# A row-wise NaN-ignoring maximum: the last tiles divided anew, and the number-free rows of 358 columns marked behind tile 52 instead of 414 behind tile 60

## The chip, the cores and the metric

The kernel runs on one core of a Trainium2 chip. The metric is the device time of one execution in microseconds (us). The core's engines work side by side and meet only at semaphores: VectorE (DVE in the profile), ScalarE (ACT), GpSimd (POOL) and SyncE (SP), which here only issues DMAs. TensorE has no work.

## The reference

```python
batch, seq, dim = 32, 2048, 2048
x = np.random.randn(batch, seq, dim).astype(np.float32)
mask = np.random.rand(batch, seq, dim) < 0.1
x[mask] = np.nan
...
return np.nanmax(x, axis=axis).astype(np.float32)     # axis = -1
```

A tenth of the 134 million elements is NaN; each of the 65,536 rows of 2048 elements gives the maximum of its numbers, and NaN if it has none. 537 MB are read, 0.26 MB written.

## The kernel before

Every one of the 128 partitions handles 512 rows. A **unit** is a quarter of a row, `Q` = 512 elements of each partition. The table `TILES` lists 74 tiles, one entry `(loads, pieces, reds)` each, all in units: the first tile has 4 units (one row), each other 28 (seven rows). The tiles go in turn through three load buffers `xt` (`BUFS`).

Each tile passes four stages.

- **Load.** SP issues one DMA for each number in `loads`. The first of them waits until the last reduction of the tile three before it has freed the buffer. Each DMA also waits for the landing of the DMA 14 before it (`LANES`).
- **Keys.** For each entry of `pieces`, ACT reads the upper 16 bits of the elements and writes a key of 16 bits into one of three key buffers `kt` (`e_key = act(...)`; the page shows it as "ACTIVATE kt<-xt"). The function has two slopes and sends every NaN to a key that later becomes a very low number.
- **Way back.** The keys are turned into upper halves again and written over the originals in `xt`. A positive number in `pieces` gives this to POOL (`pool(...)`, "TENSOR_SCALAR xt<-kt"), a negative one to ACT (`release()`, "ACTIVATE xt<-kt"). An entry in parentheses is one key step with several ways back. A negative number written as a float (`-2.0`) lets ACT make the next key first.
- **Reduction.** DVE takes the maximum over the row (`tensor_reduce`, "TENSOR_REDUCE acc<-xt") of as many units as the next number of `reds` says, as soon as all their ways back are done. The maxima of a partition stand in `acc`, one column for each row.

So `([28], [6, 10, 12], [16, 12])` is one load of 28 units, three key steps with three ways back on POOL, and reductions of four rows and of three. `([14, 14], [9, -4, 4, 4, 7], [12, 8, 8])` is two loads, and the second way back (4 units) is ACT's.

Every engine works through its instructions in the order in which the Python loop emits them; there is no planner behind it, the table is the plan. `Order` keeps the semaphores: each instruction waits only for what its engine has not yet seen. Where a reduction needs one last way back of POOL and one of ACT, `joints()` finds the two, and both then count on one semaphore of their own (`pair74_5`), so that the reduction waits once. Tiles whose number stands in `APART` are left out of that.

A row without a number ends as a very low constant in `acc` (`NONE`). `find()` marks such rows by two passes over a range of `acc`: a comparison (`none`), then an OR that makes them NaN. The tiles are split into six `GROUPS`, and a group's columns form one block of the output with one store. The marking is done behind the groups in `FLAGGED`, over all columns since the last one; group 4 (`LATE`) is marked by POOL at the very end, the last group, tile 74, by DVE. The stores of groups 0 to 3 are issued after the last load; those of groups 4 and 5 wait for their marking.

Of the kernel before, what the change touches and what calls it, by code (L numbers as in the profile page):

```python
# [15 lines left out]
TILES = (  # L16
    [([4], [4], [4])]
    + [([28], [7, 9, 12], [16, 12])] * 7
    + [([28], [9, 12, -7], [8, 20])]
    + [([28], [7, 9, 12], [16, 12])] * 7  # L20
    + [([28], [9, 12, -7], [8, 20])]
    + [([28], [7, 9, 12], [16, 12])] * 7
    + [([28], [9, 12, -7], [8, 20])]
    + [([28], [7, 9, 12], [16, 12])] * 7
    + [([28], [9, 12, -7], [8, 20])]
    + [([28], [7, 9, 12], [16, 12])] * 7
    + [([28], [9, 12, -7], [8, 20])]
    + [([28], [7, 9, 12], [16, 12])] * 7
    + [([28], [6, 10, 12], [16, 12])] * 3
    + [([28], [7, 9, 12], [16, 12])]  # L30
    + [([28], [6, 10, 12], [16, 12])] * 3
    + [([28], [7, 9, 12], [12, 16])] * 2
    + [([28], [7, 10, 11], [12, 16])]
    + [([28], [6, 10, 12], [16, 12])] * 3
    + [([28], [8, 11, 9], [8, 8, 12])]
    + [([20, 8], [11, -6, 6, 5], [16, 12])]
    + [([20, 8], [12, (-4, 7), 5], [8, 8, 12])]
    + [([17, 11], [12, (-4, 6), 6], [4, 12, 12])]
    + [([16, 12], [11, -5, 5, 7], [16, 12])]
    + [([13, 15], [9, -4, 7, 8], [12, 8, 8])]  # L40
    + [([14, 14], [9, -4, 4, 4, 7], [12, 8, 8])]
    + [([11, 10, 7], [5, 6, (-3, 7), 7], [4, 4, 4, 8, 8])]
    + [([11, 9, 8], [4, 7, (-2, 7), 6, -2], [4, 4, 4, 8, 8])]
    + [([8, 7, 6, 7], [3, 5, 7, (3, -3), 3, 4], [8, 4, 8, 8])]
    + [([6, 5, 6, 5, 6], [5, (5, -1), (-1, 5), 5, 3, 3], [4, 4, 4, 4, 4, 4, 4])]
    + [([5, 6, 5, 4, 4, 3, 1], [(-2, 3), 3, 3, (4, -1), 4, 4, -2.0, 2], [4, 4, 3, 1, 4, 4, 4, 4])]
    + [([4, 4, 3, 2, 4, 2, 3, 3, 3], [2, 2, 4, (-2.0, 1), 2, 3, 3, (-1, 2), (1, -1, 1), 2, -1.0], [4, 4, 4, 4, 4, 4, 4])]
)

GROUPS = [TILES[i : i + 15] for i in range(0, 60, 15)] + [TILES[60:73], TILES[73:]]  # L50


FLAGGED = (3, 5)
LATE = 4

APART = (70, 71, 72, 73)
WIDE = 7
BUFS = 3

# [23 lines left out]
def joints(pieces, reds):  # L83

    flat = []  # L90
    at = 0
    for step, parts in enumerate(pieces):
        for c in parts if isinstance(parts, tuple) else (parts,):

            flat.append((at, at + abs(c), c < 0, step + isinstance(c, float)))
            at += abs(c)
    needs = []
    done = 0
    for n in reds:
        over = [i for i, (a, b, _, _) in enumerate(flat) if a < done + n and b > done]  # L100
        done += n
        pools = [i for i in over if not flat[i][2]]
        backs = [i for i in over if flat[i][2]]
        if pools and backs and flat[pools[-1]][3] > flat[backs[-1]][3]:
            backs = []
        needs.append(pools[-1:] + backs[-1:])
    pairs = {}
    for need in needs:
        if len(need) == 2 and all(sum(i in n for n in needs) == 1 for i in need):
            for i in need:  # L110
                pairs[i] = tuple(need)
    return pairs
# [61 lines left out]
def kernel(  # L174
# [28 lines left out]
    of = out.bitcast(i32).flatten_outer_dims().rearrange("r c -> (r c)")  # L203
    rows = [sum(sum(loads) for loads, _, _ in g) * Q // D for g in GROUPS]
    assert R == P * sum(rows)
# [14 lines left out]
    with tc.tile_critical():  # L220
# [25 lines left out]
        def find(who, engine, deps, acc, none, op):  # L246
            e = order.add(
                who,
                engine,
                lambda: engine.tensor_scalar(  # L250
                    out=none,
                    in0=acc,
                    scalar1=NONE,
                    scalar2=float(0x00800000),
                    op0=ALU.is_equal,
                    op1=ALU.mult,
                ),
                deps,
            )
            bits = acc.bitcast(i32)  # L260
            return order.add(
                who,
                engine,
                lambda: engine.tensor_tensor(  # L264
                    out=bits, in0=bits, in1=none, op=op
                ),
                [e],
            )
# [14 lines left out]
        number = 0  # L283
# [5 lines left out]
        r0 = 0  # L289
        for gi, (s, g) in enumerate(zip(rows, GROUPS)):  # L290
            xg = xr[r0 : r0 + P * s].rearrange("(p s) d -> p (s d)", p=P)
# [5 lines left out]
            for loads, pieces, reds in g:  # L297
# [5 lines left out]
                for c in loads:  # L303
                    c *= Q
                    a, b = at, at + c
# [18 lines left out]
                part = []  # L324
                held = []
                pairs = {}
                if number not in APART:
                    pairs = joints(pieces, [n // Q for n in reds])
                flat = sum((p if isinstance(p, tuple) else (p,) for p in pieces), ())
                half = {}  # L330
# [114 lines left out]
            else:  # L445
# [3 lines left out]
                ready += [e] * (gi + 1 - len(ready))  # L449
            if gi == len(GROUPS) - 1:  # L450
                e = find("pool", nc.gpsimd, late_after, late_acc, late, ALU.add)
# [50 lines left out]
```

## Time and profile before

| | |
|---|---|
| median of 3 runs | 1251.56 us (1251.53 to 1252.36) |
| profiled execution | 1251.85 us, its span 1250.1 us |
| DVE busy | 1110.8 us (89%), 181 instructions |
| ACT busy | 965.5 us (77%), 273 instructions |
| POOL busy | 1168.7 us (93%), 242 instructions |
| read from HBM | 536.87 MB, 430 GB/s over the span |
| load of a 28-unit tile (7168 KB) | 22.6 us from issue to landing, one about every 16.9 us |

The span runs from the first to the last instruction; the execution's time also holds what lies around it, here 1.75 us. Times within a profile are counted from the start of the span. "Idle before, and who ended it" beside an instruction is the time for which its engine stood still just before it.

Three engines and the DMA queue are all close to full, so shares of the whole span say little about the end: they must be read by stretch.

### The profile page before, as it was taken

How to read it: one execution, taken by the hardware profiler on the slowest of the kernel's cores; microseconds unless marked ns; L12 is line 12 of the kernel's file. 1: busy time of each engine (PE TensorE's matmuls, PEld its weight loads, DVE VectorE, ACT ScalarE, POOL GpSimd, SP SyncE). 2: the span in 40 equal slices, each digit the busy share in tenths (PEclk: the TensorE clock that was granted, in tenths of full speed). 3: DMA queues.
4: the chain of work that ended last, by engine and by line, in shares of the span. 5: the costliest groups of instructions: out<-in, count | busy, mean ns of one | idle time of the engine just before them, and what ended most of it. 6: DMA issues, size and time to landing. Idle time of an engine off the chain costs nothing.

```text
span 1250.1 us, 886 instructions
## 1 busy us (share of the span) xinstructions
DVE 1110.8 (89%) x181; ACT 965.5 (77%) x273; POOL 1168.7 (93%) x242
## 2 busy tenths in 40 slices
DVE  0788989888889888898988888988888999999999
ACT  3777887778777877788777877777777778999998
POOL 2999989998999899998999899999999999989998
DMA  9999999999999999999999999999999999999997
GB/s 415 435 417 440 440 440 429 422 441 440 435 420 437 440 437 433 422 440 440 437 429 426 440 440 433 422 437 440 437 433 422 441 437 423 438 431 429 428 428 311
DMA packets 15991, 537.20 MB, mean 430 GB/s; under 512 B 2544, under 2 KB 2544, under 8 KB 3568
## 3 DMA queue, kind: packets, MB, share of 16 engines
q1 hardware_dynamic: 15984, 537.14, 99.4%
q14 instruction: 7, 0.06, 0.0%
HBM read 536.87 MB, written 0.26 MB: 430 GB/s over the span
## 4 chain that ended last, share of the span: by engine, by line
DMA 40%; DVE 29%; POOL 22%; ACT 9%; issue 1%; SPq 0%
DMA xt<-in_x_dram 40%; DVE acc L244 29%; POOL xt L237 22%; ACT kt L227 8%; ACT xt L227 1%; SPq L309 0%; DVE none L250 0%; DVE acc L264 0%; SPq L465 0%; SPq L220 0%
## 5 line engine op out<-in xcount | busy, mean ns | idle before, releaser
L237 POOL TENSOR_SCALAR xt<-kt 128x3584 int16<-128x3584 uint16 (+11 forms) x236 | 1167.6, 4948 | 77.6 <-ACT kt L227 63.5
L244 DVE TENSOR_REDUCE acc<-xt 128x3 f32<-128x6144 f32 (+4 forms) x175 | 1107.5, 6379 | 136.6 <-POOL xt L237 129.2
L227 ACT ACTIVATE kt<-xt 128x3584 uint16<-128x3584 int16 (+9 forms) x247 | 913.4, 3734 | 278.3 <-DMA xt<-in_x_dram 258.1
L227 ACT ACTIVATE xt<-kt 128x512 int16<-128x512 uint16 (+6 forms) x24 | 52.9, 2203 | 0.7
L227 ACT ACT_TABLE_LOAD x1 | 1.3, 1283 | 0.9 <-SPq L220 0.9
L244 DVE TENSOR_REDUCE xt<-xt 128x1 f32<-128x1536 f32 x1 | 1.7, 1742 | 0.0
L270 DVE MEMSET scalars<- 128x1 f32 x1 | 0.1, 59 | 1.0 <-SPq L220 1.0
L250 DVE TENSOR_SCALAR none<-acc 128x414 int32<-128x414 f32 (+1 forms) x2 | 0.8, 380 | 0.1
L264 DVE TENSOR_TENSOR acc<-acc,none 128x414 int32<-128x414 int32 (+1 forms) x2 | 0.7, 374 | 0.1
L250 POOL TENSOR_SCALAR late<-acc 128x91 int32<-128x91 f32 x1 | 0.5, 547 | 0.1
L264 POOL TENSOR_TENSOR acc<-acc,late 128x91 int32<-128x91 int32 x1 | 0.3, 341 | 0.1
L483 POOL MEMSET const-float32-0.0<- 128x1 f32 x1 | 0.1, 99 | 0.2 <-issue 0.2
L227 ACT ACTIVATE scalars<-scalars 128x1 f32<-128x1 f32 x1 | 0.2, 203 | 0.0
L483 POOL MEMSET const-bfloat16-1.0<- 128x1 bf16 x1 | 0.1, 102 | 0.0
L483 POOL MEMSET const-uint8-127<- 128x1 uint8 x1 | 0.1, 102 | 0.0
L483 POOL MEMSET const-float32-1.0<- 128x1 f32 x1 | 0.1, 99 | 0.0
## 6 DMA issues: line engine op xcount, KB each, us to landing
xt<-in_x_dram SPq DMA_DIRECT2D x61, 7168.0 KB, 22.6
xt<-in_x_dram SPq DMA_DIRECT2D x2, 5120.0 KB, 17.5
xt<-in_x_dram SPq DMA_DIRECT2D x3, 2816.0 KB, 22.7
xt<-in_x_dram SPq DMA_DIRECT2D x4, 2048.0 KB, 22.3
xt<-in_x_dram SPq DMA_DIRECT2D x5, 1536.0 KB, 29.1
xt<-in_x_dram SPq DMA_DIRECT2D x2, 3584.0 KB, 24.7
xt<-in_x_dram SPq DMA_DIRECT2D x6, 1024.0 KB, 26.8
xt<-in_x_dram SPq DMA_DIRECT2D x3, 1792.0 KB, 30.0
```

The lines of the kernel that those rows point to most:

```text
L227: lambda: nc.scalar.activation(**kw),
L237: lambda: nc.gpsimd.tensor_scalar(**kw),
L244: return order.add("dve", nc.vector, lambda: do(**kw), deps)
L250: lambda: engine.tensor_scalar(out=none, in0=acc, scalar1=NONE, scalar2=float(0x00800000), op0=ALU.is_equal, op1=ALU.mult,),
L264: lambda: engine.tensor_tensor(out=bits, in0=bits, in1=none, op=op),
L270: e_top = order.add("dve", nc.vector, lambda: nc.vector.memset(top, EDGE), [])
L483: nc = _bacc.Bacc("TRN2", target_bir_lowering=False, num_devices=1)
```

## The change

The rows of the table from tile 49 on are replaced. The loads of 28 units stay whole up to tile 63 (before, up to tile 62); the last tile has 12 loads instead of 9, all in all there are 107 loads instead of 105. More tiles carry ways back on ACT, among them tile 52 and tiles 57 to 66. The groups are cut at tiles 13, 26, 39, 52 and 73 instead of 15, 30, 45, 60 and 73: their columns are 85, 91, 91, 91, 147 and 7 instead of 99, 105, 105, 105, 91 and 7. So DVE marks the first 358 columns behind tile 52, where it marked 414 behind tile 60, and POOL marks 147 columns at the end instead of 91. `APART` is replaced by `PAIRED`, a list of the tiles that do use the common semaphore.

```diff
-    + [([28], [7, 9, 12], [16, 12])] * 7
-    + [([28], [6, 10, 12], [16, 12])] * 3
-    + [([28], [7, 9, 12], [16, 12])]
-    + [([28], [6, 10, 12], [16, 12])] * 3
-    + [([28], [7, 9, 12], [12, 16])] * 2
-    + [([28], [7, 10, 11], [12, 16])]
-    + [([28], [6, 10, 12], [16, 12])] * 3
-    + [([28], [8, 11, 9], [8, 8, 12])]
-    + [([20, 8], [11, -6, 6, 5], [16, 12])]
-    + [([20, 8], [12, (-4, 7), 5], [8, 8, 12])]
-    + [([17, 11], [12, (-4, 6), 6], [4, 12, 12])]
-    + [([16, 12], [11, -5, 5, 7], [16, 12])]
-    + [([13, 15], [9, -4, 7, 8], [12, 8, 8])]
-    + [([14, 14], [9, -4, 4, 4, 7], [12, 8, 8])]
-    + [([11, 10, 7], [5, 6, (-3, 7), 7], [4, 4, 4, 8, 8])]
-    + [([11, 9, 8], [4, 7, (-2, 7), 6, -2], [4, 4, 4, 8, 8])]
-    + [([8, 7, 6, 7], [3, 5, 7, (3, -3), 3, 4], [8, 4, 8, 8])]
-    + [([6, 5, 6, 5, 6], [5, (5, -1), (-1, 5), 5, 3, 3], [4, 4, 4, 4, 4, 4, 4])]
-    + [([5, 6, 5, 4, 4, 3, 1], [(-2, 3), 3, 3, (4, -1), 4, 4, -2.0, 2], [4, 4, 3, 1, 4, 4, 4, 4])]
-    + [([4, 4, 3, 2, 4, 2, 3, 3, 3], [2, 2, 4, (-2.0, 1), 2, 3, 3, (-1, 2), (1, -1, 1), 2, -1.0], [4, 4, 4, 4, 4, 4, 4])]
+    + [([28], [7, 9, 12], [16, 12])] * 10
+    + [([28], [9, 7, -1, 11], [16, 8, 4])]
+    + [([28], [7, 10, (2, 9)], [16, 12])] * 2
+    + [([28], [7, 10, (9, 2)], [16, 12])]
+    + [([28], [9, 8, (2, 9)], [16, 12])]
+    + [([28], [10, (-2, 5), 11], [8, 8, 12])]
+    + [([28], [7, (-5, 7), 9], [16, 12])]
+    + [([28], [7, (-3, 9), 9], [16, 12])]
+    + [([28], [7, (-5, 7), 9], [16, 8, 4])]
+    + [([28], [(6, 6), (5, -6), 5], [12, 16])]
+    + [([28], [9, 10, -4.0, 2, 3], [8, 8, 12])]
+    + [([28], [5, 5, 8, 6, (3, -1.0)], [4, 4, 4, 4, 8, 4])]
+    + [([17, 11], [8, (-3, 9), 8], [8, 12, 8])]
+    + [([17, 11], [8, 8, 7, -5], [4, 4, 8, 12])]
+    + [([17, 11], [8, 8, 9, -3], [8, 8, 12])]
+    + [([12, 16], [(8, -2.0), 2, 8, 8], [8, 4, 8, 8])]
+    + [([14, 14], [8, -3.0, 3, 6, 8], [8, 4, 8, 8])]
+    + [([11, 9, 8], [8, -2, 5, 5, (7, -1)], [8, 4, 8, 8])]
+    + [([10, 10, 8], [8, (-1, -1), 5, 5, (6, -2)], [8, 4, 8, 8])]
+    + [([9, 7, 4, 8], [4, (-2.0, 3), (3, 2), 2, 4, (3, -1.0), 4], [4, 8, 8, 8])]
+    + [([8, 7, 6, 7], [4, 4, 4, 3, (-2, 4), 3, 4], [4, 4, 4, 4, 4, 4, 4])]
+    + [([5, 3, 5, 3, 4, 3, 2, 3], [3, (-1, 4), 4, 4, 4, 3, -2, 3], [4, 4, 4, 4, 4, 4, 4])]
+    + [([4, 3, 1, 1, 3, 3, 2, 1, 3, 2, 2, 3], [4, 3, (-1, 1), 3, 3, -1.0, 2, 2, 3, (-1, 1), 2, -1.0], [4, 4, 4, 4, 4, 4, 4])]
...
-GROUPS = [TILES[i : i + 15] for i in range(0, 60, 15)] + [TILES[60:73], TILES[73:]]
+BOUNDS = (0, 13, 26, 39, 52, 73, 74)
+GROUPS = [TILES[a:b] for a, b in zip(BOUNDS, BOUNDS[1:])]
...
-APART = (70, 71, 72, 73)
+PAIRED = (33, 41, 57, 58, 59, 60, 64, 65, 66, 67, 68, 73, 74)
...
-                if number not in APART:
+                if number in PAIRED:
                     pairs = joints(pieces, [n // Q for n in reds])
```

## The prediction

> **What bounds the kernel now.** I began with the share of the windows, because the change touches only the stretch from tile 49 on. Columns: window, its length, busy time of VectorE (DVE), ScalarE (ACT) and GpSimd (POOL) with instructions, clock, DMA share, GB/s.
>
> ```profile
> 700.00:1038.00 338.00, 303.18 (x42) 247.84 (x60) 327.87 (x60) 1.00 1.00 434
> 1038.00:1141.00 103.00, 102.51 (x19) 97.81 (x30) 95.39 (x20) 1.00 1.00 433
> 1141.00:1204.00 63.00, 63.00 (x19) 58.37 (x26) 60.27 (x19) 1.00 1.00 429
> 1204.00:1249.00 45.00, 44.43 (x24) 39.04 (x31) 40.54 (x24) 1.00 0.86 357
> ```
>
> Up to 1204 the DMA share is 1.00: the loads set the pace and no schedule of the engines can beat them. The last load lands at 1242.63. What the engines still owe then is the part a new division can move: from there to the end of the span (1250.09) it is 7.46 us. In the last two windows DVE has no idle time either, and POOL little. The timeline tells how little (start, length, engine, operation, count, idle before it and who ended that):
>
> ```profile
> 1058.80 162.77 DVE L244 TENSOR_REDUCE acc<-xt 128x3 f32<-128x6144 f32 x40 [0.42 <-POOL xt L237]
> ...
> 1126.27 9.06 POOL L237 TENSOR_SCALAR xt<-kt 128x3584 int16<-128x3584 uint16 x2 [2.25 <-ACT kt L227]
> ...
> 1135.60 5.33 POOL L237 TENSOR_SCALAR xt<-kt 128x4608 int16<-128x4608 uint16 x1 [0.27 <-ACT kt L227]
> ...
> 1141.93 61.72 POOL L237 TENSOR_SCALAR xt<-kt 128x2048 int16<-128x2048 uint16 x19 [1.01 <-ACT kt L227]
> ...
> 1204.22 32.83 POOL L237 TENSOR_SCALAR xt<-kt 128x2560 int16<-128x2560 uint16 x16 [0.57 <-ACT kt L227]
> ...
> 1237.27 8.41 POOL L237 TENSOR_SCALAR xt<-kt 128x1536 int16<-128x1536 uint16 x6 [0.23 <-ACT kt L227]
> ```
>
> POOL waits for ACT by 0.27, 1.01, 0.57 and 0.23 us after 1126, and 0.12 once more inside the run of 19; otherwise its conversions stand 0.079 us apart. So POOL is two microseconds from being a second bound. Its prices in that stretch (groups by form, mean ns of one):
>
> ```profile
> L237 POOL TENSOR_SCALAR xt<-kt 128x3584 int16<-128x3584 uint16 x7 | 29.4, 4198 | 2.7 <-ACT kt L227 2.2
> L237 POOL TENSOR_SCALAR xt<-kt 128x2048 int16<-128x2048 uint16 x8 | 19.8, 2479 | 1.6 <-ACT kt L227 1.0
> L237 POOL TENSOR_SCALAR xt<-kt 128x1536 int16<-128x1536 uint16 x10 | 19.1, 1906 | 1.0 <-ACT kt L227 0.2
> L237 POOL TENSOR_SCALAR xt<-kt 128x2560 int16<-128x2560 uint16 x6 | 18.3, 3048 | 1.0 <-ACT kt L227 0.6
> ```
>
> The other widths have rows of the same kind: 4.772 us for 8 units (one unit is 512 elements), 3.625 for 6, 1.334 for 2, 0.765 for 1. That is about 0.571 a unit and 0.195 an instruction. Last, the end of the chain of waits: DVE, released by POOL, runs to the end.
>
> ```profile
> 1237.07 5.57 DVE acc L244 x3
> 1243.66 0.67 DVE acc L244
> 1244.33 1.52 issue
> 1245.86 2.29 DVE acc L244
> ```
>
> **The change, part by part.**
>
> *POOL's work, tiles 53 to 66.* Counting units in the table, POOL has 1964 of 2048 before and 1951 after; ACT takes 97 back instead of 84. POOL has 247 conversions instead of 236. Over the whole kernel that is 13 x 0.571 - 11 x (0.195 + 0.079) = 4.4 us less for POOL. But it comes off tiles 53 to 60 (224 units before, 209 after), where the DMA share is 1.00: worth nothing at the end.
>
> *POOL's work, tiles 67 to 74.* Here it goes the other way: tiles 68 to 74 have 170 units in 42 conversions before, 174 in 44 after, that is 4 x 0.571 + 2 x 0.274 = 2.8 us more. To see whether the waits above absorb it, I carried the durations through the new order of each engine. The load that ends tile 67 lands at 1122.98, as before (tile ends stay where they are, and the loads run without a gap). ACT converts 8 units of it in 3.61 (row of 4096), and POOL starts at 1126.70. From there POOL has 46 conversions, 2 of tile 67 and 44 of tiles 68 to 74: 6 of 8 units, 1 of 7, 2 of 6, 4 of 5, 13 of 4, 13 of 3, 5 of 2, 2 of 1. By the rows: 28.63 + 4.20 + 7.25 + 12.20 + 32.20 + 24.78 + 6.67 + 1.53 = 117.46, and 45 gaps of 0.079 make 121.0. In my carried order ACT is always ahead of it (closest at 1147, by 0.05 us; elsewhere by 0.46 us or more), so POOL never waits and ends at 1247.71. Before, it ended at 1245.69: 2.0 us later.
>
> *DVE at the end.* The elements to reduce are the same and so is DVE's total after 1141 (106.9 us, 107.0 before, each reduction less its 0.083 of overlap with the next). It is now DVE that waits, in eight places by 0.10 to 0.35 us; with the overlaps lost there, about 2 us in all. The last wait is for the conversion that completes row 5 of tile 74, four from POOL's last: 1247.71 - 1.91 - 0.77 - 1.33 - 0.24 = 1243.47. Then come three reductions of one row at 2.276 each, two of them overlapping by 0.083: 1243.55 + 6.66 = 1250.21, against 1248.13 before. The pieces for rows 6 and 7 are ready 0.15 to 0.2 us before DVE is.
>
> *Marking of number-free rows.* The two DVE passes move from 1032.86 (414 columns, 0.592 + 0.586) to behind tile 52, near 897.7, with 358 columns: in proportion 0.53 + 0.53. They fit in the wait for POOL that precedes the next tile's first reduction (1.7 us at every tile), so nothing. If that cover were gone, 1.1 us would go to the release of a load buffer, below. While the old pair ran, POOL's conversion of 5120 elements took 5.912 against 5.910 in the mean row: no contention. The Trainium skill, "SBUF — State Buffer", section "SBUF: two separate sides", has VectorE and GpSimd exclude each other over a shared port pair for some VectorE forms. By that rule 1.1 us could be added to POOL near 898; the row says it does not apply to these two passes.
>
> *The late group.* POOL's two passes at the very end have 147 columns, not 91. Rows: 0.547 + 0.341 for 91; between that and 147/91 of it, 0.9 to 1.4. They begin after 1247.7 and are over by 1249.3, their store issued by 1249.7; the last store can only start at 1250.6. Covered by 0.9 us.
>
> *Loads and stores.* Two more loads, 0.43 us of SP issue each, with 10 or more loads queued ahead: nothing. A short load costs little more than its bytes (768 KB landed 1.88 us after the one before; at 434 GB/s it is 1.81), so 0.14 us, and POOL's last conversion has 2.6 us of slack to its load. The pairs of waits (`PAIRED`) change which semaphore a reduction waits for; the nearest row is an extra wait instruction of 0.02 us on DVE, before conversions that end later anyway.
>
> *Sum.* Last reduction ends 1250.21 instead of 1248.13: +2.1 us. What follows (marking of 7 columns, store, end: 1.96) is unchanged. The profiled execution took 1251.85 with a span of 1250.1, so it goes to 1253.9; the median of the runs is 0.3 below that execution, so **1253.6**.
>
> **Rivals.** About 0.2% (2.5 us) is what a measurement of this kernel can tell from no change; the forecast, +2.1, lies within.
>
> *Slower: loads come late after tile 52.* A load starts when the tile three before it is reduced. Today it is issued 5.0 us (982.42 for a landing at 987.42) or more before the load ahead of it lands, and no gap follows. In the new order the issue slips: by my sums to 4.8 at tile 55, then 4.2, 4.1, 4.2 and 4.0, since four conversions of a 28-unit tile (4.20 + 5.91 + 1.33 + 5.34 and four gaps, 17.1 us) are longer than its load (16.9). The very first load took 4.99 from issue to landing, 2.5 of it for its bytes, so about 2.5 should be enough and the margin holds. If the queue needs 5.0, up to 1.0 us of DMA time is lost once, everything behind slides with it, and the time is 1254.6; it passes 2.5 us from a loss of 0.4. A wait of ACT that my sums put 0.05 us away adds to the same side.
>
> *No change: DVE remains the bound.* If POOL's conversions stay ahead of DVE, DVE's 106.9 us give the old end, 1251.6. For it: DVE had no idle time before. Against: POOL's own sum ends 2 us later.
>
> *Faster.* The conversions before tile 68 leave POOL 4.4 us less; were the tail POOL's alone and its start not tied to the landing at 1122.98, it would give 1249.2. The DMA share of 1.00 speaks against it.
>
> *Each load pays a fixed cost.* Two extra loads, each with the first load's 2.5 us, would give 1258.6; the spacing of 1.88 us speaks against it. The Trainium skill, "DMA: Bandwidth & Descriptors", section "Anatomy of one DMA", puts that fixed part at 2.0 us for its software path; by it the time would be 1257.6.
>
> **How the numbers follow.** Forecast 0.62 (1253.0 to 1254.3 with the scatter of the runs; a tenth of it beyond 2.5 us), late loads 0.22, DVE bound 0.09, faster 0.04, fixed cost 0.03. That gives faster 0.04, same 0.56 + 0.09 = 0.65, slower 0.06 + 0.22 + 0.03 = 0.31. The range, 1252.4 to 1255.2, takes in the late loads with scatter and part of the way to the DVE bound.
>
> **What would show it.** Right: POOL without a wait over 0.1 us from 1126.7 to 1247.7; DVE with several short waits for POOL after 1141; landings unchanged to 1242.7; the last reduction ending near 1250.2. Wrong: a landing interval over 17.3 us between 897 and 1000 (late loads), DVE unbroken after 1141 (DVE bound), or short loads landing more than 0.1 us beyond their bytes.

## The result, and the profile after

| | before | after |
|---|---|---|
| median of 20 runs | 1251.66 us (1251.53 to 1252.53) | 1254.05 us (1253.63 to 1254.63) |
| profiled execution, its span | 1251.85, 1250.1 us | 1254.04, 1252.3 us |
| last reduction ends | 1248.13 us | 1250.33 us |
| DVE instructions, busy | 181, 1110.8 us | 189, 1111.5 us |
| ACT instructions, busy | 273, 965.5 us | 290, 975.6 us |
| POOL instructions, busy | 242, 1168.7 us | 253, 1163.4 us |

The change makes the kernel 2.4 us slower, a ratio of 1.0019 (95% interval 1.0012 to 1.0026). That is small, but it is not nothing: the interval leaves out 1, and none of the 20 runs after is as short as the longest of the 20 before. So the 2.5 us that the prediction took as what a measurement can tell from no change is too wide; the interval reaches only 0.9 us to either side. POOL is busy for 5.3 us less in all and still ends later.

The shares of the windows, after, in the same columns as before (the last window is 2 us longer):

```profile
700.00:1038.00 338.00, 303.57 (x45) 262.14 (x67) 317.11 (x65) 1.00 1.00 434
1038.00:1141.00 103.00, 102.42 (x25) 94.74 (x36) 96.98 (x24) 1.00 0.99 429
1141.00:1204.00 63.00, 62.28 (x18) 57.35 (x31) 61.26 (x23) 1.00 1.01 432
1204.00:1251.00 47.00, 45.79 (x23) 39.15 (x30) 43.35 (x24) 1.00 0.83 342
```

From 700 to 1038 POOL has 10.8 us less to do (317.11, before 327.87) and ACT 14.3 more (262.14, before 247.84), but the DMA share there is 1.00, and a lighter POOL brings nothing. From 1141 to 1204 DVE, which had no idle time (63.00 of 63), now stands still for 0.7 us, and POOL has 1.0 us more work in the same 63.

The timeline of after shows it piece by piece (start, length, engine, operation, count, idle before and who ended it):

```profile
898.03 0.53 DVE L255 TENSOR_SCALAR none<-acc 128x358 int32<-128x358 f32 x1
898.60 0.53 DVE L269 TENSOR_TENSOR acc<-acc,none 128x358 int32<-128x358 int32 x1
900.29 15.15 DVE L249 TENSOR_REDUCE acc<-xt 128x4 f32<-128x8192 f32 x2 [1.16 <-POOL xt L242]
...
1126.90 120.94 POOL L242 TENSOR_SCALAR xt<-kt 128x4096 int16<-128x4096 uint16 x46 [1.94 <-ACT kt L232]
...
1141.39 57.04 DVE L249 TENSOR_REDUCE acc<-xt 128x2 f32<-128x4096 f32 x15 [0.23 <-POOL xt L242]
...
1198.62 28.63 DVE L249 TENSOR_REDUCE acc<-xt 128x2 f32<-128x4096 f32 x12 [0.19 <-POOL xt L242]
...
1227.51 11.06 DVE L249 TENSOR_REDUCE acc<-xt 128x1 f32<-128x2048 f32 x5 [0.26 <-POOL xt L242]
...
1238.84 4.48 DVE L249 TENSOR_REDUCE acc<-xt 128x1 f32<-128x2048 f32 x2 [0.27 <-POOL xt L242]
...
1243.65 6.67 DVE L249 TENSOR_REDUCE acc<-xt 128x1 f32<-128x2048 f32 x3 [0.34 <-POOL xt L242]
...
1247.93 0.73 POOL L255 TENSOR_SCALAR late<-acc 128x147 int32<-128x147 f32 x1
1248.74 0.44 POOL L269 TENSOR_TENSOR acc<-acc,late 128x147 int32<-128x147 int32 x1
```

The five rows of POOL that had waits after 1126 have become one row: 46 conversions without a wait, from 1126.90 to 1247.84. The one row of DVE has become a string of rows, each opened by a short wait for POOL. The two engines have changed roles. The marking of 358 columns stands at 898, and behind it DVE still waits 1.16 us for POOL.

POOL's conversions of that stretch, groups by form (busy, mean ns of one, idle before):

```profile
L242 POOL TENSOR_SCALAR xt<-kt 128x2048 int16<-128x2048 uint16 x13 | 32.2, 2478 | 1.0
L242 POOL TENSOR_SCALAR xt<-kt 128x4096 int16<-128x4096 uint16 x6 | 28.6, 4765 | 2.3 <-ACT kt L232 1.9
L242 POOL TENSOR_SCALAR xt<-kt 128x1536 int16<-128x1536 uint16 x13 | 24.8, 1905 | 1.0
L242 POOL TENSOR_SCALAR xt<-kt 128x2560 int16<-128x2560 uint16 x4 | 12.2, 3046 | 0.3
```

The price of one is what it was (2478 ns for 4 units, before 2479; 1905 for 3, before 1906). Only the mix differs: more pieces of 4 and 3 units.

The waits from 1126 to the end (engine, waited for: total, times, longest):

```profile
ACT kt L232 <- DMA xt<-in_x_dram: 10.8, 14, 2.8
POOL xt L242 <- ACT kt L232: 1.9, 1, 1.9
DVE acc L249 <- POOL xt L242: 1.3, 5, 0.3
```

Before, in the same stretch, POOL waited five times for ACT, 4.3 us in all, and no wait of DVE was listed. Now POOL waits once, at the start of the stretch, and DVE five times. And the end of the chain that ended last:

```profile
1242.29 1.34 POOL xt L242
1243.63 0.02 issue
1243.65 2.85 DVE acc L249 x2
1246.50 1.55 issue
1248.05 2.29 DVE acc L249
```

Before, the chain ran over DVE alone from 1237.07 to its end at 1248.53. Now it is POOL's conversions, 0.08 us apart, up to 1243.63, and three reductions behind them.

### The profile page after: what moved, and what is told of

Read it like the earlier page. It is cut to its first block, busy times and chain, and to the rows that moved or that the text cites. A ratio compares the mean times of both kernels' runs of the same rounds, so it can differ in the third digit from the quotient of the medians.

```text
span 1252.3 us, 933 instructions
## 1 busy us (share of the span) xinstructions
DVE 1111.5 (89%) x189; ACT 975.6 (78%) x290; POOL 1163.4 (93%) x253
## 4 chain that ended last, share of the span: by engine, by line
DMA 40%; DVE 25%; POOL 25%; ACT 9%; issue 1%; SPq 0%; ACTq 0%
DMA xt<-in_x_dram 40%; POOL xt L242 25%; DVE acc L249 25%; ACT kt L232 8%; ACT xt L232 1%; SPq L314 0%; DVE none L255 0%; DVE acc L269 0%; ACTq L164 0%; SPq L470 0%; SPq L225 0%
## 5 line engine op out<-in xcount | busy, mean ns | idle before, releaser
L242 POOL TENSOR_SCALAR xt<-kt 128x4608 int16<-128x4608 uint16 (+9 forms) x247 | 1162.0, 4704 | 85.4 <-ACT kt L232 70.4
L232 ACT ACTIVATE kt<-xt 128x3584 uint16<-128x3584 int16 (+10 forms) x256 | 914.8, 3610 | 268.6 <-DMA xt<-in_x_dram 241.2
L232 ACT ACTIVATE xt<-kt 128x512 int16<-128x512 uint16 (+6 forms) x32 | 61.7, 1933 | 0.8
```

What stands on the lines that cost most here:

```text
L232: lambda: nc.scalar.activation(**kw),
L242: lambda: nc.gpsimd.tensor_scalar(**kw),
```

## The experiments

Theory: the new division of tiles 67 to 74 gives POOL a queue of 121 us without a gap, and that alone sets the end. Rivals: the marking moved to tile 52, or the ways back moved to ACT in tiles 53 to 66, delay loads; ACT rather than POOL is what the end hangs on. Each kernel's time is set against runs of the kernel before on the same chip: 1251.84 us (31 runs) for the first four, 1251.85 (24) for the next four, 1251.73 (21) for the last two. Where two variants are compared that did not run on the same chip, it is by their differences from before.

**1. Only the groups and the marking.** The old table with the new bounds.

```diff
-GROUPS = [TILES[i : i + 15] for i in range(0, 60, 15)] + [TILES[60:73], TILES[73:]]
+BOUNDS = (0, 13, 26, 39, 52, 73, 74)
+GROUPS = [TILES[a:b] for a, b in zip(BOUNDS, BOUNDS[1:])]
```

> Before, with the new group bounds alone (marking of 358 columns behind tile 52, 147 columns marked by POOL at the end; table and pairs as before). Theory (the time is made by POOL's conversions of tiles 67 to 74): no change, 0.0 us, DVE unbroken to its last reduction near 1248.1. Rival (the marking delays the loads or the end): up to 1.1 us for the marking behind tile 52, 0.5 us for the wider marking at the end.

Measured: 1251.90 us, ratio 1.0001 (0.9992 to 1.0009). Its timeline ends like that of before, though POOL now marks 147 columns at the end:

```profile
1237.12 8.40 POOL L239 TENSOR_SCALAR xt<-kt 128x1536 int16<-128x1536 uint16 x6 [0.20 <-ACT kt L229]
1245.60 0.73 POOL L252 TENSOR_SCALAR late<-acc 128x147 int32<-128x147 f32 x1
```

Within the scatter, the marking and the groups cost nothing (+0.06 us).

**2. Only the new tail.** The old kernel with the new rows of tiles 67 to 74.

```diff
-    + [([13, 15], [9, -4, 7, 8], [12, 8, 8])]
...
-    + [([4, 4, 3, 2, 4, 2, 3, 3, 3], [2, 2, 4, (-2.0, 1), 2, 3, 3, (-1, 2), (1, -1, 1), 2, -1.0], [4, 4, 4, 4, 4, 4, 4])]
+    + [([12, 16], [(8, -2.0), 2, 8, 8], [8, 4, 8, 8])]
...
+    + [([4, 3, 1, 1, 3, 3, 2, 1, 3, 2, 2, 3], [4, 3, (-1, 1), 3, 3, -1.0, 2, 2, 3, (-1, 1), 2, -1.0], [4, 4, 4, 4, 4, 4, 4])]
-APART = (70, 71, 72, 73)
+APART = (69, 70, 71, 72)
```

> Before, with tiles 67 to 74 alone in the new division (marking, bounds and tiles 49 to 66 as before). Theory: the whole loss, +2.0 to +2.4 us, POOL without a wait from about 1126.8 to 1247.8, DVE's last reduction ending near 1250.3. Rival (tiles 49 to 66 or the late release of load buffers carry part of it): less than 1.5 us.

Measured: 1253.90 us, +2.06, ratio 1.0016 (1.0008 to 1.0025). POOL's row in the timeline:

```profile
1126.79 121.07 POOL L237 TENSOR_SCALAR xt<-kt 128x4096 int16<-128x4096 uint16 x46 [1.92 <-ACT kt L227]
```

POOL ends at 1247.86 and the last reduction at 1250.33, both as in the changed kernel. The tail by itself carries 2.06 of the 2.39 us. The other 0.33 show in no trace: the profiled executions of this kernel and of the changed one took 1254.05 and 1254.04 us, and the kernel before has 1251.84 here and 1251.66 where the change was measured.

**3. Everything but the new tail.** The changed kernel with the old rows of tiles 67 to 74.

```diff
-    + [([12, 16], [(8, -2.0), 2, 8, 8], [8, 4, 8, 8])]
...
-    + [([4, 3, 1, 1, 3, 3, 2, 1, 3, 2, 2, 3], [4, 3, (-1, 1), 3, 3, -1.0, 2, 2, 3, (-1, 1), 2, -1.0], [4, 4, 4, 4, 4, 4, 4])]
+    + [([13, 15], [9, -4, 7, 8], [12, 8, 8])]
...
+    + [([4, 4, 3, 2, 4, 2, 3, 3, 3], [2, 2, 4, (-2.0, 1), 2, 3, 3, (-1, 2), (1, -1, 1), 2, -1.0], [4, 4, 4, 4, 4, 4, 4])]
-PAIRED = (33, 41, 57, 58, 59, 60, 64, 65, 66, 67, 68, 73, 74)
+PAIRED = (33, 41, 57, 58, 59, 60, 64, 65, 66, 67, 68, 74)
```

> After, with tiles 67 to 74 in the old division (marking, bounds and tiles 49 to 66 new). Theory: the time of before, within 0.3 us, with POOL's old waits of 0.2 to 1.0 us back and DVE unbroken. Rival (tiles 49 to 66 carry part of it): +0.5 to +1.5 us.

Measured: 1252.58 us, +0.74, ratio 1.0006 (0.9997 to 1.0015): more than the theory gave. The old waits of POOL are back and POOL's long queue is gone, but the timeline has two waits that the kernel before does not have:

```profile
1232.89 4.73 POOL L242 TENSOR_SCALAR xt<-kt 128x2048 int16<-128x2048 uint16 x3 [0.60 <-ACT kt L232]
...
1235.40 13.32 DVE L249 TENSOR_REDUCE acc<-xt 128x1 f32<-128x2048 f32 x6 [0.38 <-POOL xt L242]
```

Behind them stands a load that lands at 1228.38, 0.68 us later than its bytes ask for by the spacing of the others. At 1226.5 the DMA engines carried one packet of 8192 bytes of the queue "instruction". In the kernel before there is such a packet at 1245.5, after the last load, and none among the last loads. So a new rival: code that the engines fetch takes its turn among the loads. DVE's end is 0.58 us later than before: it starts its last run 0.10 later, waits 0.38, and loses the overlap of 0.08. The rest of the 0.74 lies outside the span (execution less span is 1.9 us, 1.75 before).

**4. Four more conversions of POOL, the same units.** The changed kernel with four pieces of tiles 68 and 69 cut in two.

```diff
-    + [([14, 14], [8, -3.0, 3, 6, 8], [8, 4, 8, 8])]
-    + [([11, 9, 8], [8, -2, 5, 5, (7, -1)], [8, 4, 8, 8])]
+    + [([14, 14], [8, -3.0, 3, (3, 3), (4, 4)], [8, 4, 8, 8])]
+    + [([11, 9, 8], [8, -2, (3, 2), (2, 3), (7, -1)], [8, 4, 8, 8])]
```

> After, with four ways back of POOL in tiles 68 and 69 cut in two (6 into 3 and 3, 8 into 4 and 4, 5 into 3 and 2, 5 into 2 and 3): the same units, four conversions more. Theory (POOL's unbroken run sets the end): 4 x (0.195 + 0.079) = +1.1 us over after, all of it at the end; the run from 1126.9 then has 50 conversions in 122.0 us. Rival (DVE is the bound, or ACT, POOL only looks full): 0.0 us over after.

Measured: 1255.05 us, +3.21, which is 0.82 more than the change itself; ratio 1.0026 (1.0016 to 1.0036).

```profile
1126.66 121.99 POOL L242 TENSOR_SCALAR xt<-kt 128x4096 int16<-128x4096 uint16 x50 [1.90 <-ACT kt L232]
```

POOL's run is 1.05 us longer (four times 0.195 + 0.079 make 1.10), started 0.24 earlier in this profile, and the last reduction ends 0.80 later, at 1251.13. Every added tenth of POOL in this stretch reaches the end.

**5. The new packet moved away?** Experiment 3 with a common semaphore in three more tiles, so that the instruction streams have another length.

```diff
-PAIRED = (33, 41, 57, 58, 59, 60, 64, 65, 66, 67, 68, 74)
+PAIRED = (9, 17, 25, 33, 41, 57, 58, 59, 60, 64, 65, 66, 67, 68, 74)
```

> The kernel of the third experiment (after, with tiles 67 to 74 in the old division), with tiles 9, 17 and 25 put back on the common semaphore, as before: no unit, conversion or reduction differs, only which semaphores a few instructions of the first third wait for. In the third experiment a packet of 8,192 bytes of the queue named instruction came at 1226.5, the loads behind it landed late, and POOL waited 0.6 us at 1232.9. Theory (that packet, not tiles 49 to 66, made the 0.74 us over before): the packet moves to where it is before the change (385 in the first third, past 1242 at the end), the last loads land as before, and the time goes back to that of before within 0.3 us. Rival (tiles 49 to 66 carry it): still +0.6 to +0.8 us.

Measured: 1252.53 us, +0.68, ratio 1.0006 (0.9997 to 1.0015). A packet of the first third moved, from 434 to 385, but the late one stayed, at 1226.8; the load behind it landed 0.48 late and POOL waited 0.40. Inconclusive: what should have moved did not, so the run does not tell the two theories apart.

**6. POOL relieved by three units.** One way back of tile 68 goes from POOL to ACT.

```diff
-    + [([14, 14], [8, -3.0, 3, 6, 8], [8, 4, 8, 8])]
+    + [([14, 14], [8, -3.0, -3, 6, 8], [8, 4, 8, 8])]
```

> After, with 3 units of tile 68 moved from POOL to ACT (the third way back). Theory that POOL's units alone make the loss: POOL has 1.98 us less to do, so -1.5 to -2.0 us against after. Theory that the order of ACT and POOL together make it (ACT converts 0.05 to 0.5 us ahead of POOL there, and a way back of 1.92 us put between two keys makes the next key late): POOL waits for ACT by about 3 us in tile 68 or 69, and the time is +1.0 us against after.

Measured: 1255.11 us, +3.26, 0.87 more than the change itself; ratio 1.0026 (1.0016 to 1.0037).

```profile
1127.06 14.45 POOL L242 TENSOR_SCALAR xt<-kt 128x4096 int16<-128x4096 uint16 x3 [1.94 <-ACT kt L232]
...
1144.48 104.46 POOL L242 TENSOR_SCALAR xt<-kt 128x3072 int16<-128x3072 uint16 x42 [2.97 <-ACT kt L232]
```

ACT's rows ahead of that wait:

```profile
1138.14 3.65 ACT L232 ACTIVATE xt<-kt 128x1536 int16<-128x1536 uint16 x2
1141.66 9.75 ACT L232 ACTIVATE kt<-xt 128x3072 uint16<-128x3072 int16 x3
```

POOL's conversions take 118.91 us instead of 120.94, 2.03 less, but POOL stands still for 2.97 us in between, and its start was 0.15 later: it ends 1.09 later. ACT works in order; the way back it was given comes ahead of the key that POOL needs next. That key begins at 1141.66, in the changed kernel at 1140.08, and POOL, which has one conversion less, is free for it at 1141.51 instead of 1143.34. The theory that POOL's sum alone decides falls here: the end hangs on POOL's queue together with the order of ACT that feeds it, not on POOL's sum alone. In the changed kernel the table gets ACT just far enough ahead that POOL never waits.

**7 and 8. The marking three and six times.** How much room the loads behind tile 52 have.

```diff
-                e = find(
-                    "dve", nc.vector, after, accs[:, lo:flagged], nones[:, lo:flagged], ALU.bitwise_or
-                )
+                for _ in range(3 if gi == 3 else 1):      # 6 in the second kernel
+                    e = find(
+                        "dve", nc.vector, after, accs[:, lo:flagged], nones[:, lo:flagged], ALU.bitwise_or
+                    )
+                    after = [e]
```

Expected of three times:

> After, with the marking behind tile 52 done three times (the second and third change nothing), so that the load of tile 56 and the following are released later by about 2.1 us. If a load needs to be issued about 2.5 us before the one ahead of it lands: no gap, 0.0 us. If it needs the 5.0 us that the trace of before showed as its least: a gap of 1 us or more in the landings and the time +1 us or more against after.

Expected of six times:

> After, with the marking behind tile 52 done six times, 5.4 us more of VectorE in one place. Theory (loads are issued with about 4 us to spare of which 2.5 are needed; what is lost in the loads reaches the end in full): a gap of about 2.8 us in the landings near tile 56 and +2.8 us against after. Rival (buffers or the tail take up the delay): less than 1 us.

Measured with three: 1254.12 us, +2.27, ratio 1.0018 (1.0009 to 1.0027), the same as the change itself. The load that waits for tile 53 is issued 3.25 us before the load ahead of it lands (916.20 for 919.45), and it lands 17.36 us after it, as in the changed kernel (17.33), so no gap comes of it.

Measured with six: 1256.88 us, +5.03, ratio 1.0041 (1.0029 to 1.0054), 2.6 more than the change itself. The same load is issued at 919.60, 0.14 us after the landing ahead of it, and its own landing at 939.36 is 3.0 us late. ACT, which waits for it, and the end of POOL's queue show what becomes of that:

```profile
939.38 7.55 ACT L232 ACTIVATE kt<-xt 128x4608 uint16<-128x4608 int16 x2 [6.27 <-DMA xt<-in_x_dram]
```

```profile
1129.70 120.98 POOL L242 TENSOR_SCALAR xt<-kt 128x4096 int16<-128x4096 uint16 x46 [1.84 <-ACT kt L232]
```

POOL starts its run of 46 at 1129.70 instead of 1126.90, 2.8 us later, and the last reduction ends 2.8 later. Time of the DMA queue that is lost at 920 is lost at the end, nearly in full (2.8 of 3.0 us). By this run a load needs about 2.9 us ahead (939.36 less 16.9 for its bytes is 922.46, 2.86 after its issue); the changed kernel has 4.1 or more. This is an estimate, if anything too high: an instruction packet at 921.1 falls into this load too, and no run has a lead between 3.25 us and none. The Trainium skill, "DMA: Bandwidth & Descriptors", section "Anatomy of one DMA", gives about 2.0 us fixed for its software path; these loads go out by the queue "hardware_dynamic", and the 2.9 is for them.

**9. A longer program, the same work.** The kernel before, with nine tiny instructions more on each of ACT, DVE and POOL at its start. They write columns that nothing reads.

```diff
+        for i in range(2, 11):
+            u, v, w = (scalars[:, i + n : i + n + 1] for n in (0, 10, 20))
+            act([e_top], out=u, in_=top, func=ACT.Prelu, alpha=0.5)
+            order.add("dve", nc.vector, lambda: nc.vector.memset(v, 0.0), [])
+            order.add("pool", nc.gpsimd, lambda: nc.gpsimd.memset(w, 0.0), [])
```

> Before, with nine tiny instructions more on each of ACT, POOL and DVE at the start, while they wait for the first load (they write unused columns; no wait, conversion or reduction differs). In the runs with tiles 67 to 74 in the old division and the rest new, a packet of the queue named instruction came at 1226.5 to 1226.8, the load behind it landed 0.5 to 0.7 us late, and the time was 0.7 us over before; in before that packet comes at 1245.5, behind the last load. Theory (a longer program brings this packet forward among the last loads, and there it costs): the packet comes before 1240, a load behind it lands 0.5 us late, POOL waits for it, and the time is +0.4 to +0.7 us over before. Rival (the division of tiles 49 to 66 cost those 0.7 us): 0.0 us.

Measured: 1252.32 us, +0.59, ratio 1.0004 (0.9995 to 1.0013). The packet of 1245.5 now comes at 1231.4; five others come 51 to 74 us earlier, and the one at 1129.8 stays. The DMA queues from 1228 to 1240 (packets, MB, share of 16 engines) have a row that the kernel before does not have there:

```profile
q1 hardware_dynamic: 965, 5.05, 101.2%
q14 instruction: 1, 0.01, 0.2%
```

and the timeline has the waits that follow from it:

```profile
1237.82 8.39 POOL L237 TENSOR_SCALAR xt<-kt 128x1536 int16<-128x1536 uint16 x6 [1.05 <-ACT kt L227]
...
1239.76 8.87 DVE L244 TENSOR_REDUCE acc<-xt 128x1 f32<-128x2048 f32 x4 [0.67 <-POOL xt L237]
```

A load lands at 1233.79, 0.75 late; POOL waits 1.05 us where it waited 0.23, DVE 0.67 where it did not wait, and the last reduction ends 0.50 later. At the start nothing is lost: tile 67 lands at 1122.73, before at 1122.97. So the place of the instruction packet is worth about half a microsecond in the old tail, with no change to the table at all. The interval of the ratio takes in 1, here as in experiments 3 and 5. But 20 of the 21 runs of the kernel before are shorter than the shortest of these 11, in experiments 3 and 5 all of them are, and the profile shows where the time goes.

**10. The old tail and the old tiles 53 to 60.** Experiment 3 with these rows put back too.

```diff
-    + [([28], [7, 10, (2, 9)], [16, 12])] * 2
...
-    + [([28], [7, (-5, 7), 9], [16, 8, 4])]
+    + [([28], [6, 10, 12], [16, 12])] * 3
+    + [([28], [7, 9, 12], [12, 16])] * 2
+    + [([28], [7, 10, 11], [12, 16])]
+    + [([28], [6, 10, 12], [16, 12])] * 2
-PAIRED = (33, 41, 57, 58, 59, 60, 64, 65, 66, 67, 68, 74)
+PAIRED = (33, 41, 64, 65, 66, 67, 68, 74)
```

> The kernel of the third experiment with tiles 53 to 60 in the old division too: new are only the group bounds, tiles 49 to 52 and tiles 61 to 66. Eight instructions or more are gone from the program ahead of the end. Theory of the packet: it comes later than 1226.5; if past the last load (1242.6) the time is that of before within 0.3 us, else between that and +0.7. Rival (the ways back on ACT in tiles 53 to 60 cost 0.7 us): the time is that of before with the packet still at 1226.

Measured: 1252.89 us, +1.16, ratio 1.0010 (1.0001 to 1.0018). The packet comes at 1231.6, a load lands at 1234.00, 0.74 late, POOL waits 1.01 for it at 1238.04, and the last reduction ends 0.71 later than before. That is the loss of experiment 9 (0.50 there), somewhat larger. Most of the other 0.4 us are not in the span: execution less span is 2.1 us here, against 1.75 in the kernel before. The three kernels with the new rows of tiles 61 to 66 and the old tail have 1.93 (experiment 3), 1.98 (5) and 2.09 (10), all others 1.75 or 1.76. What this is stays open; the packet alone does not make it, as experiment 9 has the packet and 1.75. The new ways back of tiles 53 to 60 are not what experiment 3 lost: they are gone here, and more is lost, not less.

## Why the prediction came out as it did

**POOL's queue: right.** Forecast were 46 conversions from 1126.70 to 1247.71, 121.0 us; measured are 46 from 1126.90 to 1247.85, 120.94. No wait within them, as forecast. Experiment 2 shows that the eight rows of the tail are enough for this, and experiment 4 that the end follows POOL's queue nearly tenth by tenth. From 1245.69 to 1247.85 the end of the queue moves by 2.16 us, and the rows give three parts: POOL starts 0.63 later (mainly because ACT's first key of tile 67's last load has 8 units, before 7), has 3.3 us more of conversions and gaps, and no longer has 1.8 us of waits for ACT.

**DVE's new waits: right.** Eight waits after 1141, of 0.09 to 0.34 us; forecast eight of 0.10 to 0.35. The last three reductions start at 1243.65 (forecast 1243.55) and end at 1250.33 (forecast 1250.21).

**ACT always ahead: right, and tighter than it reads.** Nothing in the changed kernel waits there (at 1147 ACT's key is done at 1146.99 and POOL is free at 1147.05, 0.06 later; forecast 0.05). But experiment 6 shows what it hangs on: one way back of 1.9 us moved from POOL into ACT's queue behind 1138 gives POOL a wait of 3 us. "Four units more on POOL" is the right cause of the loss; moving units off POOL is not by itself the cure.

**Marking: right.** Two passes of 0.53 us behind tile 52, and DVE still waits 1.16 us after them. They do not slow POOL: a conversion of 1024 elements that lies wholly beside the six markings of experiment 8 took 1.327 us, the mean of its like is 1.329. The late group takes 0.73 + 0.44 = 1.17 us (forecast 0.9 to 1.4), is over at 1249.18, its store is issued at 1249.54 and the last store starts at 1250.75. Experiment 1 has both at no cost.

**Late loads, the rival of 0.22: not what happened, though its test struck.** The leads (from a load's issue to the landing of the load ahead of it) came as worked out: 4.8 us at tile 55, then 4.3, 4.5, 4.3, 4.1 (forecast 4.2, 4.1, 4.2, 4.0). Landings between 897 and 1000 stand 16.88 to 16.92 us apart, but one interval is 17.33, just beyond the 17.3 that was to count against the forecast. A lead of 4.3 us cannot be its cause, since in experiment 7 the same load has a lead of 3.25 and the same interval (17.36), and in experiment 10 a lead of 4.86 and nearly the same (17.21). An instruction packet at 923.4 falls into that load; the kernel before has the same in its load of 953.64 (0.36 late, packet at 940.0). The test could not tell a late issue from a disturbed transfer. The rival's mechanism exists, as experiment 8 shows: it sets in below 3.25 us of lead, by the estimate there at about 2.9, not at 5.0.

**"Landings unchanged to 1242.7": wrong.** The last load landed at 1243.46, 0.8 late, and a load at 1213.72 was 0.68 late with an instruction packet at 1212.0. So the sign "short loads landing more than 0.1 us beyond their bytes" struck too, and not because of a fixed cost. Not all of the 0.8 is the packet's: in experiment 2, without a packet among the last loads, the last one landed at 1243.24. The delays cost nothing, because POOL's queue never ran empty. The old tail has no such slack, which is why the same disturbance shows in experiments 3, 5, 9 and 10. That is also why the parts do not add up (+2.06 for the tail, +0.74 for the rest, +2.39 together), though only 0.58 of the 0.74 lie inside the span.

**Two more loads: no fixed cost.** From tile 67's landing to the last one it is 119.66 us before and 120.00 in experiment 1, which has the same loads, and 120.23 in experiment 2. There the new tail has three loads more; in the changed kernel tile 63 has one less, which makes two in all. None of the three has an instruction packet among the last loads. The three loads together cost 0.6 us at most, where the rival's 2.5 apiece would make 7.5. The forecast of 0.07 apiece cannot be resolved within that.

**The size: 0.45 us short.** Of this 0.14 are in the profile: execution 1254.04, forecast 1253.9, mainly because tile 67 landed 0.15 later than before. (Tile 49 already landed 0.28 later, where the rows of the table are still the old ones.) The other 0.31 is a step of the sum: it took the median of the runs to lie 0.3 below the profiled execution, as it did in the three runs shown. After, median and profiled execution agree (1254.05, 1254.04), and over 20 runs of the kernel before the distance is 0.19. A profiled execution is one draw, and its distance from the median does not carry over to another kernel.

## What to carry to other kernels

Cost a change to a schedule in the stretch where its engine is the bound: POOL lost 5.3 us of work over the kernel and the time rose by 2.4, because the work came off a stretch that DMA paces and about 3 us were added to the last one. When two engines are within 2 us of each other, work that is shifted from one to the other must be followed in the order of the queues, as the sum of each engine does not say who will wait (experiment 6). Differences of up to about 0.6 us can come from the length of the program alone (experiment 9); repeat a kernel with a few idle instructions more before a difference of that size is put down to the edit.

## What the runs showed of the hardware

The trace has packets of 8192 bytes of a queue "instruction", by its name the engines' code: seven within the span in the kernels before and after, six in experiment 2. They take their turn among the loads, and most delay the landing of the load that they fall into: 0.36 us in before (packet at 940.0), 0.43 in after (923.4), 0.68 in experiment 3 (1226.5), 0.75 in experiment 9 (1231.4). Not every one does: behind the one at 978.2 in after the interval is 16.89 us, as elsewhere. Why is not settled.

At the rate of all 16 engines these bytes would be 0.02 us. But the packet itself takes 0.31 us, and the packet of the load that starts just as it ends takes longer than its like: at 923.69 in after 2.36 us instead of 2.12 for 57,344 bytes, at 1226.77 in experiment 3 0.84 instead of 0.31 for 8192. Together that is 0.56 and 0.84 us, enough for the delays of 0.43 and 0.68. That the two packets share one DMA engine, and that a load lands when its slowest engine is done, is inferred from these times.

Experiment 9 shows that the length of the program decides where most of the packets fall. Which engine's code they are was not settled; the one at 1129.8 stayed at 1129.83 in experiment 9, which adds instructions to ACT, DVE and POOL and none to SyncE. The Trainium skill, "Runtime: NRT & Kernel Launch", section "Instruction fetch mechanics", has each sequencer fetch its code by a DMA queue of its own while it executes, and calls the fetch hidden. The queue is in the trace (packets of the kind "instruction"). What the runs show is another cost than an engine's wait for its code: it delays loads, and that shows in the time where the last ones come late.
